# Four edits of instruction order in a two-layer decoder trunk: the sums and the rotary tables of the feed-forward, the end of the stick-breaking mixer, and 42 transposes of the identity at the start

## The chip, the cores and the metric

The kernel runs on one core of a Trainium2 chip. The metric is the device time of one execution, in microseconds (us); lower is better. A core has five instruction queues that matter here: PE (TensorE, matrix products, with its weight loads shown apart as PEld), DVE (VectorE), ACT (ScalarE), POOL (GpSimd) and SP (SyncE, which issues every DMA of this kernel). Each queue runs its instructions in the order in which they were written out when the kernel was built; an instruction waits at the head of its queue until what it reads is there and what it overwrites is free.

## The reference

Two layers over 512 tokens of width 1024, everything in float32. Layer 0 mixes tokens by retention (with rotary tables), layer 1 by stick-breaking attention. Around each mixer stand two half-step feed-forwards, and each layer ends with a gated embedding:

```python
for i in range(DEPTH):
    f = swiglu(rmsnorm(h, g[0]), w_gate[i, 0], w_up[i, 0], w_down[i, 0])
    h = h + 0.5 * rmsnorm(f, g[1])
    m = retention(...) if i % 2 == 0 else stick_breaking(...)
    h = h + rmsnorm(m, g[3])
    f = swiglu(rmsnorm(h, g[4]), w_gate[i, 1], w_up[i, 1], w_down[i, 1])
    h = h + 0.5 * rmsnorm(f, g[5])
    gate = sigmoid(rmsnorm(h, g[6]) @ ple_w_gate[i])
    h = h + rmsnorm(gate * (p[i] @ ple_w_proj[i]), g[7])
```

with `swiglu(x, ...) = (silu(x @ w_gate) * (x @ w_up)) @ w_down` and a hidden width of 2816. `rmsnorm` divides each token by the root of the mean of its squares and multiplies by a gain.

## The kernel before

**Products.** A float32 product is made of three float32r products (`mm3`, L157 to L161): each operand is split into a high part, copied by ACT (L153), and a low part, subtracted by DVE (L154). Weights come in tiles of 128x1024 (512 KB) by DMA into eight `raw` buffers, and are split into `wh` and `wl` (`piece`), of which five pairs of buffers exist (`HL_BUFS`); `_load` makes the pieces in the order of a list of items, and `_ahead` makes as many as there are free buffers. The four token tiles t = 0 to 3 hold 128 tokens each.

**Feed-forward.** `ffn` runs four times. The first hidden pair is computed plainly from four weight tiles, the other ten pairs by seven products on half-size blocks (Strassen's scheme, in Winograd's form). A pair has four raw weight tiles; products 1, 2, 3 use three of them as they are, product 4 a difference that is made late, and products 5, 6, 7 use sums of them: `t1` = raw - raw, then two more sums in place of two raw tiles. These three sums (1024 wide, on DVE, in `_load`, L247) are made just ahead of the piece of product 6, which is third in a pair's order (1, 2, 6, 5, 7, 3, 4). One product is 24 PE matmuls of 256 columns. PE adds up several products in one PSUM bank, ACT and DVE take the banks over to `y` (L687) and to the gated hidden value `u` (L748).

**Norms.** Between two parts of a layer stands a chain per token tile: DVE adds the last partial product to `part` (`close_a` for its first half, L558, and `close_b` for its second, L565), ACT squares it, POOL makes the reciprocal root (L526 to L541; it also multiplies the first half by the gain, L528), DVE multiplies the second half by the gain (L539) and adds the residual (L546), and then `pre` does the same for the next part's input norm: ACT square (L460), POOL (L451, L452), DVE `xn` (L464), PE transposes of `xn` (L470), ACT and DVE split of the transposed tile into `xs`.

**What sets the order.** A scheduler places the instructions by a model of their times; PE's order is written by hand wherever `traced()` stands. `issue_after(x)` makes what follows stand behind x on x's engine, with no wait. `chained()` gives the norm chains priority and keeps each engine's part of them in the written order. `gates` holds instructions behind which the next pieces must stand. `rope_tables` (L392 to L446) makes the sine and cosine tables with 24 DVE operations of 512 columns and three of ACT, and stores them by two DMAs that retention later reads; the scheduler puts it where it finds room. Its tiles share buffers with `xn` and `rin`.

**Start.** `run` loads the four token tiles, does `pre` for t = 0 and 1, transposes both (`flush`), sets the gates there, and then does `pre` for t = 2 and 3, whose transposes stand behind the second and the third weight tile (`_wstat_halves`).

**Stick-breaking end.** `last_products` multiplies the eight heads' outputs `oT` by the output weights. Its `product(half, t, heads)` adds some heads to the bank of one half of one token tile, one `mm3` of 512 columns for each head. In the order before, all four tiles get heads 4 to 6 of half 0, `context(7)` makes the last head, tile 0 gets heads 2 to 6 of half 1, then all four tiles get head 7 of half 0, each with its `close_a`; after that half 1 is finished tile by tile with `close_b`.

Of the kernel before, what the change touches and what calls it, by code (L numbers as in the profile page):

```python
# [18 lines left out]
P = 128  # L19
D = 1024  # L20
S = 512
NT = S // P
# [58 lines left out]
class Trunk:  # L81
# [148 lines left out]
    def piece(self, x, w, home=None):  # L230
        if home and home[0] == "blk":
            parts = [self.blk2() for _ in range(2)]
            for i, hl in enumerate(parts):
                self.split(hl, x[:, i * 512 : i * 512 + 512])
            return tuple(Parts(p) for p in zip(*parts))
        if home and home[0] in ("xe", "xs"):
            h, l = (getattr(self, home[0])[:, 2 * home[1] + i] for i in range(2))
        elif home:
            h, l = (self.work.tile([P, 1280], F32R, tag="pk", name="pk", bufs=self.npacks)[:, :w] for _ in range(2))
        else:  # L240
            h = self.hl.tile([P, 1024], F32R, tag="wh", name="wh")[:, :w]
            l = self.hl.tile([P, 1024], F32R, tag="wl", name="wl")[:, :w]
        self.split((h, l), x)
        return h, l

    def sub(self, out, a, b, op=ALU.subtract):
# [2 lines left out]
    def _load(self):  # L249
        n = self.loaded  # L250
        item = self.items[n]
        self._open(n)
        if item[0] == "w":
            x = self.packs.pop(n)
            self.queue[n] = self.piece(x, 1024, self.home.get(n))
        elif item[0] == "st":
            _, key, prod = item
            b = self.packs[key]
            if prod == 6:
                w = b[0, 0].shape[-1]  # L260
                b["t1"] = self.sums.tile([P, 1024], F32, tag="t1", name="t1")[:, :w]

                with self.tc.issue_after(self.s_sums):
                    self.sub(b["t1"], b[0, 1], b[0, 0])
                    self.sub(b[0, 0], b[1, 1], b["t1"])
                    self.sub(b[0, 1], b[1, 1], b[0, 1])
            x = {1: b[0, 0], 2: b[1, 0], 3: b[1, 1], 4: b[0, 0], 5: b.get("t1"), 6: b[0, 0], 7: b[0, 1]}[prod]
            self.queue[n] = self.piece(x, x.shape[-1])
            if prod == 6:
                self.sub(b[0, 0], b[1, 0], b[0, 0])  # L270
        self.loaded += 1
# [85 lines left out]
    def setup(self):  # L357
        nc, tc = self.nc, self.tc
        c = self.cpool


        self.part = [c.tile([P, D], F32, name=f"part{t}") for t in range(NT)]
        self.keep = [self.dram.tile([P, D], F32, name=f"keep{t}") for t in range(NT)]
        self.src = [self.ins["x"][t * P : (t + 1) * P, :] for t in range(NT)]
        self.trig = [self.dram.tile([P, 512], F32, name=f"trig{t}") for t in range(2)]
        x = self.xs.rearrange("p (t q d) (c k) -> p t q d c k", t=2, q=2, c=4)
        self.xT = [x[:, :, :, d] for d in range(2)]
        self.ident = c.tile([P, P], F32, name="ident")
        make_identity(nc, self.ident)
        self.mhalf = c.tile([P, 1], F32, name="mhalf")  # L370
        nc.gpsimd.memset(self.mhalf, -0.5)
        self.junk = c.tile([P, 512], BF16, name="junk")
        self.gng = c.tile([P, RH * RDV // P], F32, name="gng")
        self.inv = c.tile([P, 1], F32, name="inv")

    def triangle(self):
        nc = self.nc
# [307 lines left out]
    def ffn(self, layer, j, gpost, after, side=None):  # L685
# [102 lines left out]
        with self.traced():  # L788
            for n, x in enumerate(ffn_steps()):
                if n == 50 and side:  # L790
                    side()
                (gate_up if x[0] == "gu" else down)(*x[1:])
                if x[:2] == ("gu", NPAIR - 1) and x[2] in ORDER[2:]:
                    self.open_home(self.LAST[ORDER.index(x[2]) - 2])
# [191 lines left out]
    def stick(self, layer, gpost, after):  # L986
# [143 lines left out]
        h = SH - 1  # L1130

        def last_products():
# [8 lines left out]
            def product(half, t, heads):  # L1141
                for hd in heads:
                    h0 = 4 - 2 * half
                    u = (us0, us1)[half][(hd - h0) // 2]
                    self.mm3(pss[half][t], stat(hd)(0, t), [x[:, hd % 2, :] for x in u], hd == h0, hd == h)

            for t in range(NT):
                product(0, t, range(4, h))
            context(h)
            product(1, 0, range(2, h))  # L1150
            for t in range(NT):
                product(0, t, (h,))
                ssa[t] = self.close_a(t, pss[0][t], gpost, False)
            self.done_with(2)
            for t in range(NT):
                if t:
                    product(1, t, range(2, SH - 3))
                self.run_c()
# [68 lines left out]
    def run(self):  # L1227
# [10 lines left out]
        x(3)  # L1238
        nc.sync.dma_start(out=self.gng, in_=self.ins["gn"])
        nc.sync.dma_start(out=self.inv, in_=self.ins["inv"])  # L1240
        for t in range(NT):
            with self.chained():
                self.pre(t, g, True)
            self.run_d()
            if t == 1:
                self.flush()
                self.gates, self.gated = list(self.ends.values()), 3
        self.layers()
        assert self.at == len(self.items), (self.at, len(self.items))

# [99 lines left out]
```

## Time and profile before

| what | before |
|---|---|
| device time, median of 3 (range) | 2220.15 us (2218.29 to 2221.09) |
| profiled execution: its time, its span | 2220.81 us, 2218.9 us |
| mean granted PE clock in it | 0.995 |
| PE / PEld busy | 2174.7 us / 1962.7 us |
| DVE / ACT / POOL busy | 1466.0 us / 1003.4 us / 236.7 us |
| weights and activations read, written | 229.38 MB, 17.30 MB |

The profile is one execution on the chip. Rows of its timeline give the start (us from the start of the span), the duration, the engine, the line of the kernel, the operation with its output and inputs, how many equal instructions the row joins, and in square brackets how long the engine idled before and which instruction ended that. Rows of waits give the waiting engine and line, what it waited for, and the sum, the number and the longest of these waits. Rows of windows give the busy time of each engine in a stretch, the granted PE clock (PEclk, 1.00 is full speed), the share of the DMA engines and GB/s.

### The profile page before, as it was taken

How to read it: one execution, taken by the hardware profiler on the slowest of the kernel's cores; microseconds unless marked ns; L12 is line 12 of the kernel's file. 1: busy time of each engine (PE TensorE's matmuls, PEld its weight loads, DVE VectorE, ACT ScalarE, POOL GpSimd, SP SyncE). 2: the span in 40 equal slices, each digit the busy share in tenths (PEclk: the TensorE clock that was granted, in tenths of full speed). 3: DMA queues.
4: the chain of work that ended last, by engine and by line, in shares of the span. 5: the costliest groups of instructions: out<-in, count | busy, mean ns of one | idle time of the engine just before them, and what ended most of it. 6: DMA issues, size and time to landing. Idle time of an engine off the chain costs nothing.

```text
span 2218.9 us, 32989 instructions
## 1 busy us (share of the span) xinstructions
PE 2174.7 (98%) x13640; PEld 1962.7 (88%) x13640; DVE 1466.0 (66%) x1739; ACT 1003.4 (45%) x1476; POOL 236.7 (11%) x337
## 2 busy tenths in 40 slices
PE   8999999999999999999999999999999989999998
PEld 7899998888888899999988999998988889999986
DVE  7976676553535588577766976776554568767764
ACT  5543444232223355344555544444555455444443
POOL 0000003110111210000032000002131220000031
PEclk9999999999999999999999999999999999999999
DMA  5323335231322324322453233235312232333341
GB/s 214 127 102 97 106 121 181 91 106 60 110 76 81 124 96 134 114 97 94 143 201 131 87 116 112 98 103 171 115 58 77 86 115 95 105 105 105 114 162 57
DMA packets 69415, 248.83 MB, mean 112 GB/s; under 512 B 7952, under 2 KB 7952, under 8 KB 69264
## 3 DMA queue, kind: packets, MB, share of 16 engines
q1 hardware_dynamic: 69264, 246.72, 33.6%
q8 instruction: 107, 1.75, 0.3%
q14 instruction: 44, 0.36, 0.1%
HBM read 229.38 MB, written 17.30 MB: 111 GB/s over the span
## 4 chain that ended last, share of the span: by engine, by line
PE 88%; DVE 6%; ACT 2%; issue 1%; POOL 1%; DMA 1%; SPq 0%; DVEq 0%; POOLq 0%; ACTq 0%
PE ps L728 33%; PE ps L160 18%; PE ps L159 18%; PE ps L161 18%; PE ps L1042 1%; DVE wl L154 1%; DMA raw<-wts 1%; DVE raw L247 1%; DVE xs L154 1%; PE ps L470 1%; DVE part L546 0%; DVE xe L154 0%; DVE y L687 0%; ACT xn L460 0%; POOL st L541 0%
## 5 line engine op out<-in xcount | busy, mean ns | idle before, releaser
L154 DVE TENSOR_TENSOR wl<-raw,wh 128x1024 fp32r<-128x1024 f32 x427 | 526.6, 1239 | 356.2 <-ACT wh L153 353.5
L153 ACT ACTIVATE wh<-raw 128x1024 fp32r<-128x1024 f32 x427 | 449.8, 1059 | 640.5 <-PE ps L728 202.2
L728 PE MATMUL ps<-xs,wh 128*128 128x256 f32 x2560 | 464.7, 283 | 6.7 <-DVE y L687 6.6
L728 PEld LDWEIGHTS ps<-xs,wh 128*128 128x128 f32 x2560 | 399.0, 189 | 11.0 <-DVE y L687 7.9
L728 PE MATMUL ps<-xs,wl 128*128 128x256 f32 x1280 | 362.9, 284 | 0.0
L728 PE MATMUL ps<-xe,wh 128*128 128x256 f32 x1920 | 350.5, 284 | 0.0
L728 PEld LDWEIGHTS ps<-xe,wh 128*128 128x128 f32 x1920 | 302.3, 193 | 1.9
L728 PE MATMUL ps<-xe,wl 128*128 128x256 f32 x960 | 272.8, 284 | 4.3 <-DVE wl L154 4.3
L159 PE MATMUL ps<-wh,blk 128*128 128x512 f32 x680 | 266.3, 392 | 1.9 <-ACT blk L153 1.9
L161 PE MATMUL ps<-wh,blk 128*128 128x512 f32 x680 | 265.2, 391 | 1.1 <-DVE blk L154 1.1
L160 PE MATMUL ps<-wl,blk 128*128 128x512 f32 x680 | 266.0, 391 | 0.0
L728 PEld LDWEIGHTS ps<-xs,wl 128*128 128x128 f32 x1280 | 242.3, 189 | 0.0
L728 PEld LDWEIGHTS ps<-xe,wl 128*128 128x128 f32 x960 | 184.9, 193 | 4.5 <-DVE wl L154 4.5
L160 PE MATMUL ps<-xs,wh 128*128 128x256 f32 (+1 forms) x576 | 186.1, 323 | 2.2 <-DVE xs L154 2.2
L159 PE MATMUL ps<-xs,wh 128*128 128x256 f32 (+1 forms) x576 | 186.5, 324 | 0.2 <-ACT xs L153 0.2
L161 PE MATMUL ps<-xs,wl 128*128 128x256 f32 (+1 forms) x576 | 185.3, 322 | 0.0
L161 PE MATMUL ps<-wh,xs 128*128 128x512 f32 (+1 forms) x448 | 162.9, 364 | 0.0
L159 PE MATMUL ps<-wh,xs 128*128 128x512 f32 (+1 forms) x448 | 162.7, 363 | 0.0
L160 PE MATMUL ps<-wl,xs 128*128 128x512 f32 (+1 forms) x448 | 162.6, 363 | 0.0
L526 POOL TENSOR_SCALAR st<-st 128x1 f32<-128x1 f32 x32 | 8.9, 279 | 1375.0 <-ACT junk L524 1358.9
L161 PEld LDWEIGHTS ps<-wh,blk 128*128 128x128 f32 x680 | 128.0, 188 | 28.7 <-DVE blk L154 1.5
L159 PEld LDWEIGHTS ps<-wh,blk 128*128 128x128 f32 x680 | 128.2, 189 | 26.8 <-ACT blk L153 2.1
(169 smaller groups left out, 3443.8 us busy)
## 6 DMA issues: line engine op xcount, KB each, us to landing
raw<-wts SPq DMA_DIRECT2D x382, 512.0 KB, 3.5
keep<-part SPq DMA_DIRECT2D x28, 512.0 KB, 4.2
rin<-keep SPq DMA_DIRECT2D x28, 512.0 KB, 4.1
gbc<-gains SPq DMA_DIRECT2D x16, 512.0 KB, 3.8
part<-x SPq DMA_DIRECT2D x4, 512.0 KB, 7.7
rin<-x SPq DMA_DIRECT2D x4, 512.0 KB, 4.9
out<-part SPq DMA_DIRECT2D x8, 256.0 KB, 2.2
dec<-decay SPq DMA_DIRECT2D x4, 256.0 KB, 3.7
```

The source lines that it names most:

```text
L153: h = self.nc.scalar.activation(hl[0], x, AF.Copy)
L154: l = self.nc.vector.tensor_tensor(out=hl[1], in0=x, in1=hl[0], op=ALU.subtract)
L159: mm(ps, a[0], b[0], start=start, stop=False)
L160: mm(ps, a[0], b[1], start=False, stop=False)
L161: mm(ps, a[1], b[0], start=False, stop=stop)
L247: self.nc.vector.tensor_tensor(out=out, in0=a, in1=b, op=op)
L470: nc.tensor.transpose(ps[:, c * P : (c + 1) * P], xn[:, (4 * q + c) * P : (4 * q + c + 1) * P], self.ident)
L526: nc.gpsimd.tensor_scalar(out=r, in0=ss, scalar1=1.0, scalar2=(4 if half else 1) * RMS_EPS, op0=ALU.mult, op1=ALU.add)
L728: nc.tensor.matmul(o, w[a][:, g, k, :], x[b][:, k, :], start=new and g + k + n == 0, stop=k == 3 and n == 2, skip_group_check=True)
L1042: nc.tensor.matmul(ps, l, m, start=fresh and i == 0, stop=i == len(pairs) - 1, skip_group_check=True)
```

## The change

Four things are changed, and none of them changes a value that is computed. The number of instructions stays the same but for 42 transposes.

1. The three sums of a pair stand behind the low split of the piece made last before them.
2. `rope_tables` stands behind the last hidden split that was written before it.
3. `last_products` has another order, and `close_a`, `run_c`, `close_b` and `run_d` follow each other per token tile.
4. At the start PE's order is by hand: 24 transposes of the identity into a PSUM bank that nobody reads, then tile 0 is transposed, 14 more such transposes, tile 1, 4 more. `pre` of tile 1 now stands behind tile 0's transposes and their split, and the gates are taken after all four `pre`.

```diff
 def piece(self, x, w, home=None):
...
         self.split((h, l), x)
+        self.last_piece = self.split_ins[1].ins
...
 def _load(self):
...
-                with self.tc.issue_after(self.s_sums):
+                with self.tc.issue_after(self.s_sums), self.tc.issue_after(self.last_piece):
...
+    def warm(self, n):
+        ps = self.ps()
+        for i in range(n):
+            self.nc.tensor.transpose(ps[:, i % 4 * P : i % 4 * P + P], self.ident, self.ident)
...
 def ffn(self, layer, j, gpost, after, side=None):
...
                 if n == 50 and side:
-                    side()
+                    with ExitStack() as stack:
+                        for i in self.split_ins:
+                            stack.enter_context(self.tc.issue_after(i.ins))
+                        side()
...
 def last_products():
...
             for t in range(NT):
-                product(0, t, range(4, h))
+                product(0, t, (4, 5))
+            for t in range(2):
+                product(0, t, (6,))
+            product(1, 0, range(2, 6))
             context(h)
-            product(1, 0, range(2, h))
+            for t in range(2, NT):
+                product(0, t, (6,))
+            product(1, 0, (6,))
             for t in range(NT):
                 product(0, t, (h,))
+                if t == NT - 1:
+                    self.done_with(2)
                 ssa[t] = self.close_a(t, pss[0][t], gpost, False)
-            self.done_with(2)
-            for t in range(NT):
                 if t:
                     product(1, t, range(2, SH - 3))
                 self.run_c()
...
 def run(self):
...
-        for t in range(NT):
-            with self.chained():
-                self.pre(t, g, True)
-            self.run_d()
-            if t == 1:
-                self.flush()
-                self.gates, self.gated = list(self.ends.values()), 3
+        with self.traced():
+            self.warm(24)
+            for t in range(NT):
+                with self.chained():
+                    self.pre(t, g, True)
+                self.run_d()
+                if t < 2:
+                    self.flush()
+                    self.warm(14 - 10 * t)
+            self.gates, self.gated = list(self.ends.values()), 3
```

The lines of the changed kernel are numbered 1 to 15 higher; a number behind a name below tells one buffer from another.

The order of DVE at the start, before: `xn` is the normed input of a token tile (`part0` to `part3`), `wl` the low part of a weight tile.

```order
L464 SCALAR_TENSOR_TENSOR xn_127<-part0_92,st_129,gbc_113 128x1024
L464 SCALAR_TENSOR_TENSOR xn_134<-part1_93,st_136,gbc_113 128x1024
L154 TENSOR_TENSOR wl_203<-raw_116,wh_202 128x1024
L154 TENSOR_TENSOR xs_58<-ps_140,xs_58 128x4x128
L154 TENSOR_TENSOR xs_58<-ps_147,xs_58 128x4x128
L154 TENSOR_TENSOR xs_58<-ps_154,xs_58 128x4x128
L154 TENSOR_TENSOR xs_58<-ps_161,xs_58 128x4x128
L154 TENSOR_TENSOR wl_207<-raw_118,wh_206 128x1024
L154 TENSOR_TENSOR wl_211<-raw_120,wh_210 128x1024
L464 SCALAR_TENSOR_TENSOR xn_169<-part2_94,st_171,gbc_113 128x1024
L464 SCALAR_TENSOR_TENSOR xn_176<-part3_95,st_178,gbc_113 128x1024
L154 TENSOR_TENSOR wl_215<-raw_192,wh_214 128x1024
```

The same place on DVE after the change:

```order
L471 SCALAR_TENSOR_TENSOR xn_154<-part0_92,st_156,gbc_113 128x1024
L154 TENSOR_TENSOR xs_58<-ps_160,xs_58 128x4x128
L154 TENSOR_TENSOR xs_58<-ps_167,xs_58 128x4x128
L471 SCALAR_TENSOR_TENSOR xn_190<-part1_93,st_192,gbc_113 128x1024
L154 TENSOR_TENSOR wl_251<-raw_116,wh_250 128x1024
L154 TENSOR_TENSOR xs_58<-ps_196,xs_58 128x4x128
L154 TENSOR_TENSOR xs_58<-ps_203,xs_58 128x4x128
L471 SCALAR_TENSOR_TENSOR xn_216<-part2_94,st_218,gbc_113 128x1024
L471 SCALAR_TENSOR_TENSOR xn_223<-part3_95,st_225,gbc_113 128x1024
L154 TENSOR_TENSOR wl_255<-raw_118,wh_254 128x1024
L154 TENSOR_TENSOR wl_259<-raw_120,wh_258 128x1024
L154 TENSOR_TENSOR wl_263<-raw_240,wh_262 128x1024
```

The split of tile 0 now stands ahead of `xn` of tile 1, and the second, third and fourth weight tile are split behind `xn` of tile 3, where two of them stood ahead of `xn` of tile 2.

In the first feed-forward, DVE before, at the sums of pairs 1 and 2 (`t1_766` and raw 393 to 399 belong to pair 2, raw 194 to 200 and `wl_598` to pair 1; `wl_598` is the low part for product 6 of pair 1):

```order
L247 TENSOR_TENSOR t1_766<-raw_397,raw_393 128x1024
L435 TENSOR_TENSOR rope_2242<-rope_2242,rope_2244 128x512
L247 TENSOR_TENSOR blk_517<-blk_517,blk_516 128x512
L154 TENSOR_TENSOR xe_91<-blk_516,xe_91 128x4x128
L247 TENSOR_TENSOR raw_194<-raw_200,t1_593 128x1024
L247 TENSOR_TENSOR raw_198<-raw_200,raw_198 128x1024
L247 TENSOR_TENSOR raw_393<-raw_399,t1_766 128x1024
L247 TENSOR_TENSOR raw_397<-raw_399,raw_397 128x1024
L406 TENSOR_SCALAR rope_2242<-rope_2242 128x512
L154 TENSOR_TENSOR xe_91<-blk_517,xe_91 128x4x128
L687 TENSOR_TENSOR y_707<-y_707,ps_709 128x512
L154 TENSOR_TENSOR wl_598<-raw_194,wh_597 128x1024
```

The same place after the change (pair 1 has `t1_641`, raw 242 to 248 and `wl_646`; pair 2 has `t1_814` and raw 441 to 447):

```order
L248 TENSOR_TENSOR t1_641<-raw_246,raw_242 128x1024
L154 TENSOR_TENSOR xe_91<-blk_564,xe_91 128x4x128
L154 TENSOR_TENSOR xe_91<-blk_565,xe_91 128x4x128
L248 TENSOR_TENSOR raw_242<-raw_248,t1_641 128x1024
L248 TENSOR_TENSOR raw_246<-raw_248,raw_246 128x1024
L154 TENSOR_TENSOR wl_646<-raw_242,wh_645 128x1024
L154 TENSOR_TENSOR wl_683<-t1_641,wh_682 128x1024
L248 TENSOR_TENSOR raw_242<-raw_244,raw_242 128x1024
L154 TENSOR_TENSOR wl_719<-raw_246,wh_718 128x1024
L154 TENSOR_TENSOR wl_752<-raw_248,wh_751 128x1024
L694 TENSOR_TENSOR y_755<-y_755,ps_757 128x512
L154 TENSOR_TENSOR wl_783<-raw_242,wh_782 128x1024
```

Pair 2's sums and the rotary operations no longer stand between pair 1's sums and its first low part. Pair 2's `t1` is the next row after these. In the later pairs the sums stand behind the low part of the pair's own product 2 (or of a down-projection tile written just before), where some stood four to six pieces earlier. The rotary operations now stand between the pieces of a pair some 150 DVE rows further on, and the two DMAs that store the tables some 40 rows further on in SP's queue.

At the stick-breaking end, POOL before (L528 multiplies the first half of a token tile by the gain; L540 and L541 make the reciprocal root of the mixer's closing norm, L451 and L452 that of the next input norm):

```order
L526 TENSOR_SCALAR st_16719<-st_16717 128x1
L528 TENSOR_TENSOR part0_92<-part0_92,gbc_14667 128x512
L526 TENSOR_SCALAR st_16728<-st_16726 128x1
L528 TENSOR_TENSOR part1_93<-part1_93,gbc_14667 128x512
L526 TENSOR_SCALAR st_16737<-st_16735 128x1
L528 TENSOR_TENSOR part2_94<-part2_94,gbc_14667 128x512
L526 TENSOR_SCALAR st_16746<-st_16744 128x1
L528 TENSOR_TENSOR part3_95<-part3_95,gbc_14667 128x512
L540 TENSOR_TENSOR st_16758<-st_16757,st_16719 128x1
L541 TENSOR_TENSOR st_16758<-st_16758,mhalf_107 128x1
```

POOL after the change:

```order
L533 TENSOR_SCALAR st_16767<-st_16765 128x1
L535 TENSOR_TENSOR part0_92<-part0_92,gbc_14715 128x512
L547 TENSOR_TENSOR st_16775<-st_16774,st_16767 128x1
L548 TENSOR_TENSOR st_16775<-st_16775,mhalf_107 128x1
L533 TENSOR_SCALAR st_16786<-st_16784 128x1
L535 TENSOR_TENSOR part1_93<-part1_93,gbc_14715 128x512
L458 TENSOR_SCALAR st_16804<-st_16801 128x1
L459 TENSOR_TENSOR st_16804<-st_16804,mhalf_107 128x1
L547 TENSOR_TENSOR st_16819<-st_16818,st_16786 128x1
L548 TENSOR_TENSOR st_16819<-st_16819,mhalf_107 128x1
```

The reciprocal root of tile 0 stands behind one multiplication by the gain, where it stood behind four.

## The prediction

> **What bounds the kernel now.** I read the page's busy times first, then the table of waits of PE over the whole run (the sum of the waits, their number, the longest).
>
> ```profile
> span 2218.9 us, 32989 instructions
> PE 2174.7 (98%) x13640; PEld 1962.7 (88%) x13640; DVE 1466.0 (66%) x1739; ACT 1003.4 (45%) x1476; POOL 236.7 (11%) x337
> ...
> PE ps L470 <- DVE xn L464: 15.0, 4, 8.1
> PE ps L728 <- DVE y L687: 6.6, 5, 2.5
> PE ps L728 <- DVE wl L154: 4.3, 1, 4.3
> PE ps L159 <- ACT blk L153: 3.5, 5, 1.9
> PE ps L161 <- DVE blk L154: 1.1, 1, 1.1
> ```
>
> PE is busy for 98% of the span, and the change takes no product away. So an order can win only what PE idles (2218.9 - 2174.7 = 44 us, and of these 8.1 before its first work) and what it runs at a lower clock. The waits shown, 30.5 us, are nearly all of what is within reach; all four places that the change touches are among them. The clock is read from windows of 20 us:
>
> ```profile
> 60.00:80.00 20.00, 15.72 (x113) 15.51 (x112) 19.49 (x25) 10.40 (x14) 0.00 (x0) 0.83 0.32 106
> 1760.00:1780.00 20.00, 18.90 (x82) 15.70 (x82) 8.99 (x12) 6.42 (x14) 2.98 (x4) 0.91 0.31 106
> 1780.00:1800.00 20.00, 14.30 (x65) 11.45 (x64) 11.51 (x14) 6.61 (x14) 10.12 (x16) 0.91 0.45 138
> 1860.00:1880.00 20.00, 17.48 (x135) 17.28 (x134) 17.73 (x22) 8.76 (x14) 0.00 (x0) 0.92 0.34 106
> ```
>
> The eighth column is the clock. Taken as stretches at half speed these are 0.17 x 40 = 6.8 us, 3.6, 3.6 and 3.2 us; work in such a stretch loses half its length. Each stands at one of the waits below: where PE idles for some 2 us or more the clock falls, and the wait is paid a second time. I add 2.7 us for the first (1.5 of its 6.8 lie in the idle time), 1.4 and 1.6 for the two of the stick-breaking end, 1.6 for the last.
>
> **Edit 1 and 2, first feed-forward.** Around PE's longest wait in the middle of the run stand these rows of DVE and PE:
>
> ```profile
> 32.00:66.00 34.00, 6.87 (x12) 0.00 (x0) 1.00 0.10 32
> 57.65 2.37 DVE L247 TENSOR_TENSOR t<-raw 128x1024 f32<-128x1024 f32 x2
> 61.72 1.24 DVE L247 TENSOR_TENSOR raw<-raw,t 128x1024 f32<-128x1024 f32 x1
> 65.13 1.24 DVE L247 TENSOR_TENSOR raw<-raw 128x1024 f32<-128x1024 f32 x1
> 67.80 1.24 DVE L154 TENSOR_TENSOR wl<-raw,wh 128x1024 fp32r<-128x1024 f32 x1
> 69.09 0.58 PE L728 MATMUL ps<-xe,wl 128*128 128x256 f32 x1 [4.28 <-DVE wl L154]
> ```
>
> The first row is the rotary tile alone: 6.87 us of DVE in 34 us (its first number is DVE). The low part for product 6 begins at 67.80, and PE stood from 64.81 to 69.09 for it. Ahead of it stand the rotary operations and pair 2's three sums (half of the two t and of four raw rows: 3 x 1.2 = 3.6 us). Both leave this place: 6.9 + 3.6 = 10.5 us less, of which some is taken up where DVE now waits for PE's banks; even at 5 us the low part is ready before PE asks. So the wait of 4.28, a later one of 0.3 and the clock's 2.7 go: **-7.2 us**.
>
> Where the tables go, DVE has room:
>
> ```profile
> 200.00:260.00 60.00, 60.00 (x416) 56.16 (x415) 42.56 (x50) 25.50 (x34) 0.00 (x0) 1.00 0.31 98
> L410 DVE SCALAR_TENSOR_TENSOR rope<-rope x10: 686/694/706, 30.1 to 74.9; 128x512 f32<-128x512 f32 x10
> SPq L445 <- ACT rope L441: 2.6, 1, 2.6
> ```
>
> PE is busy for all 60 us there and DVE for 42.56. The tables are 10 x 0.69 and 14 shorter ones, 13 us in all, against 17.4 of slack: I cost them at nothing. If the cover fails, DVE's excess is paid at PE, 2 to 4 us; and SP's two stores wait for the last table with weight loads queued behind them (2.6 us before, the third row), which eight raw buffers cover. The bound is 0 to +4.
>
> **Edit 1, the other three feed-forwards.** Here the trace has waits of DVE for a DMA and, a few instructions later, of PE for DVE:
>
> ```profile
> 1252.26 1.23 DVE L247 TENSOR_TENSOR t<-raw 128x1024 f32<-128x1024 f32 x1 [2.55 <-DMA raw<-wts]
> 1255.27 0.51 PE L728 MATMUL ps<-xs,wh 128*128 128x256 f32 x2 [1.71 <-DVE y L687]
> 1271.31 0.50 PE L728 MATMUL ps<-xs,wh 128*128 128x256 f32 x2 [1.45 <-DVE y L687]
> ...
> DVE t L247 <- DMA raw<-wts: 2.8, 2, 2.3
> PE ps L728 <- DVE y L687: 2.5, 1, 2.5
> ```
>
> The last two rows are of 1845 to 1885. In each case a later pair's `t1` stands at the head of DVE before its weights have landed; the additions to `y` behind it come late, and PE waits for the bank that they read. Behind the change `t1` stands where its pair's product 2 is already split, so its raw tiles are due anyway. Gains: 1.71 + 1.45 = 3.2; 2.5 and the clock's 1.6; and 0.6 in the second feed-forward, what is left of the row of 6.6 (6.6 - 3.2 - 2.5 - 0.3). Sum **-7.9 us**. What is late next: the three sums and the low part follow each other just ahead of product 6, 4 x 1.22 = 4.9 us. A product is 24 matmuls at 0.12 us, 2.9 us, and five pairs of buffers let a piece be made four products ahead, 11.5 us. The chain fits with some 6 us over.
>
> **Edit 3, the stick-breaking end.** Rows of PE, DVE and POOL:
>
> ```profile
> 1759.29 0.50 PE L159 MATMUL ps<-wh,blk 128*128 128x512 f32 x1 [1.92 <-ACT blk L153]
> 1761.13 0.79 PE L161 MATMUL ps<-wh,blk 128*128 128x512 f32 x1 [1.10 <-DVE blk L154]
> 1776.97 1.30 POOL L528 TENSOR_TENSOR part<-part,gbc 128x512 f32<-128x512 f32 x1
> 1782.25 1.30 POOL L528 TENSOR_TENSOR part<-part,gbc 128x512 f32<-128x512 f32 x1
> 1777.89 0.69 DVE L565 TENSOR_TENSOR part<-part,ps 128x512 f32<-128x512 f32 x1
> 1784.36 1.28 DVE L546 SCALAR_TENSOR_TENSOR part<-part,st,rin 128x1024 f32<-128x1024 f32 x1 [3.89 <-POOL st L541]
> 1789.50 1.06 PE L470 MATMUL ps<-ident,xn 128*128 128x128 f32 x8 [3.50 <-DVE xn L464]
> 1794.86 1.97 PE L470 MATMUL ps<-ident,xn 128*128 128x128 f32 x8 [2.21 <-DVE xn L464]
> ```
>
> From tile 0's last addition (1777.89) to its transposes (1789.50) pass 11.6 us, because POOL multiplies all four tiles by the gain (1776.97 to 1783.55) ahead of the first root; DVE idles 3.89 us for that root. With one multiplication ahead of it this part shrinks by some 3.9 us to 7.7. The last addition also comes earlier: three one-head products of 0.68 us fewer ahead of it, the wait of 3.0 before head 6 cut to some 0.6 (nine more products stand before it now), and the clock's 1.4: 2.0 + 2.4 + 1.4 = 5.8, at 1772. So tile 0 is ready near 1780, where PE gets to it near 1781: no wait. Tile 1 follows 5.4 us after tile 0 before (1794.86 - 1789.50), and will be ready some 1.2 us late. Of all that PE loses here, 1.9 + 1.1 + 3.5 + 2.2 = 8.7 idle and 3.0 of clock, I leave 0.6 at head 6, 1.2 at tile 1 and 1.0 at the split behind it: **-8.9 us**. Bounds: 0 (what is late next takes it all) and -11.7 (all of it goes).
>
> **Edit 4, the start.** DVE, ACT and PE:
>
> ```profile
> 9.97 1.29 DVE L464 SCALAR_TENSOR_TENSOR xn<-part,st,gbc 128x1024 f32<-128x1024 f32 x1 [1.97 <-POOL st L452]
> 14.89 2.36 DVE L154 TENSOR_TENSOR wl<-raw,wh 128x1024 fp32r<-128x1024 f32 x2
> 15.71 1.05 ACT L460 ACTIVATE xn<-part 128x1024 f32<-128x1024 f32 x1
> 19.97 1.28 DVE L464 SCALAR_TENSOR_TENSOR xn<-part,st,gbc 128x1024 f32<-128x1024 f32 x1 [0.71 <-POOL st L452]
> 11.32 1.97 PE L470 MATMUL ps<-ident,xn 128*128 128x128 f32 x8 [1.29 <-DVE xn L464]
> 19.90 0.27 PE L159 MATMUL ps<-xs,wh 128*128 128x256 f32 x1
> 22.40 1.03 PE L470 MATMUL ps<-ident,xn 128*128 128x128 f32 x8
> ```
>
> Eight transposes take 1.97 us early and 1.03 at 22.40: PE runs at half speed until 19.9. The 42 transposes, 42 x 0.25 = 10 us at half speed, mostly fill time that PE idles (8.1 us before tile 0, and the wait for tile 1), and can bring full speed forward. But the weights are now the later ones. Tile 1's square stands behind tile 0's split: at 9.7 for 7.87, so `xn` 1 at 11.8, its transposes at 13.1 and the first product at 14.4 or so. Tiles 2 and 3 are squared one behind the other from 14.7, `xn` of tile 3 ends at 20.2, and only then comes the second `wl`: done at 21.3 where it was done at 16.1 (the row of two at 14.89). Product 1 (24 matmuls) is over by 18 at full speed and by 20 at half, so PE waits for 21.3 either way. The third weight tile then starts near 24.9 for 23.2: **+1.7 us** at full speed. As PE idles for 1 to 3 us just there, the clock is likely down after it, for up to 3.4 us more (the stretches above): another 1.7. I take **+2.5**, bounds 0 and +5.
>
> The Trainium skill, "TensorE: Matmul & The Clock Gate", part 4 (PE-mode transpose), says that transposes do not count as busy time for the clock. By that rule the 42 would change nothing but the queue, the first product would run at half speed, and the start would cost about +3.4 in place of +1.7. This trace speaks rather against it: the eight transposes from 1794.86 are 1.97 us, more than half of the 3.6 us at half speed there, and the clock was full again behind them.
>
> **Sum.** -7.2 - 7.9 - 8.9 + 2.5 = -21.5 us against the profiled execution's 2220.81, so 2199.3; the median of the three runs is 0.7 lower than that execution. Predicted: **2199 us**.
>
> **Rivals.**
> (a) *The sums just in time meet something else.* In the feed-forwards the waits for `y` move to the low part of product 6, since `t1` now also stands behind a low split that waits for a buffer. For it: DVE is busy 17.73 of 20 us at 1860 to 1880. Against it: 6 us of cover. Then edit 3 and the first feed-forward alone pay, and the tables cost 3: -8.9 - 7.2 + 2.5 + 3 = -10.6: 2210 us.
> (b) *The end's wait only moves.* Tile 1 is late by as much as tile 0 was, since DVE and ACT now interleave both halves of three tiles. The end then gives 5.8 - 2 = some 4 us: 2204 us.
> (c) *Slower.* The chain of three sums and a low part, 4.9 us, is paid in each of 40 pairs. It decides from the point where pieces are made less than two products (5.7 us) ahead; with one product ahead (2.9) it costs 2.0 a pair, 40 x 2.0 = 80 us, less the 13 that is won elsewhere: some 2286 us. At 1252 the pieces were ahead by more than that in spite of 2.55 us of waiting, so it is unlikely.
> (d) *The edits do not do what they say*: the scheduler's order keeps a wait of the same length at each of the three places, and the start costs: 2222 us.
>
> **How the numbers follow.** Forecast 0.62, (a) 0.13, (b) 0.13, (c) 0.05, (d) 0.07. The forecast's own bounds are the sum with the end at -11.7 and the start at 0 (2194) and with the start at +5 and the tables at +4 (2206). (a) and (b) reach to 2211; low 2193 and high 2212 leave out (c), (d) and little else. About 0.2%, 4.4 us, is what a measurement of this kernel can tell from no change: faster means below 2215.7. Forecast, (a) and (b) are all faster: 0.88; (d) is no change, 0.07; (c) slower, 0.05.
>
> **What would show it.** Right: no wait of PE near 65 us, none for `y` in the later feed-forwards, at the stick-breaking end tile 0's transposes near 1772 (8.5 us from the parts before, 9 here) with no wait ahead of them; POOL's first root behind one multiplication. At the start a new wait of PE for `wl` of 1 to 3 us near 18 to 21, and the third tile's transposes some 2 us later than 22.40. Wrong: a wait of PE for `wl` ahead of product 6, a wait near 200 to 260, weight loads late behind the tables' stores, or a start that is no later than before.

## The result, and the profile after

| | before | after |
|---|---|---|
| device time, median | 2219.4 us (4 runs, 2218.29 to 2221.09) | 2198.59 us (4 runs, 2197.71 to 2198.9) |
| ratio to before, 95% interval | | 0.9905 (0.9888 to 0.9922) |
| span of the profiled execution | 2218.9 us | 2196.8 us |
| PE busy; the rest of the span | 2174.7; 44.2 us | 2171.3; 25.5 us |
| DVE / ACT / POOL busy | 1466.0 / 1003.4 / 236.7 us | 1460.2 / 1002.4 / 236.7 us |

The kernel is 20.8 us faster, 0.9%. The time sits in the parts where the forecast put it. First the waits of PE over the whole run after the change (the sum, the number, the longest); L477, L735 and L572 are L470, L728 and L565 of before.

```profile
PE ps L477 <- DVE xn L471: 5.0, 3, 2.5
PE ps L161 <- DVE wl L154: 2.9, 1, 2.9
PE ps L159 <- ACT xs L153: 1.7, 2, 1.5
PE ps L159 <- ACT blk L153: 1.6, 4, 0.4
PE ps L160 <- DVE xs L154: 1.5, 6, 0.3
```

The rows of 6.6 us (for `y`) and 4.3 us (for product 6's low part) are gone, that of 15.0 us (for `xn`) is 5.0, and one is new: 2.9 us for a `wl`, at the start. To see where the 22 us of span went, I subtract the times at which the same transposes of `xn` run in the two traces; they stand at every border between parts. The row is that of tile 3, or of tile 0 where it says so; a negative number is time won:

| border | before, us | after, us | difference | made in this part | forecast |
|---|---|---|---|---|---|
| start | 27.59 | 31.38 | +3.8 | +3.8 | +2.5 |
| end of feed-forward 1 (tile 0) | 363.97 | 359.30 | -4.7 | -8.5 | -7.2 |
| end of feed-forward 2 (tile 0) | 1124.58 | 1119.09 | -5.5 | -0.9 | -0.6 |
| end of feed-forward 3 (tile 0) | 1537.38 | 1528.13 | -9.2 | -3.8 | -3.2 |
| end of stick-breaking | 1810.47 | 1792.69 | -17.8 | -8.5 | -8.9 |
| end of feed-forward 4 (tile 0) | 2143.26 | 2121.14 | -22.1 | -4.3 | -4.1 |

In the parts that the change leaves alone (retention, the two embeddings) the difference moves by less than 0.1 us; that is why a row of the fourth column can differ from the next by 0.1 more or less than the fifth says. Timeline rows of the first feed-forward after the change, and the window into which the tables moved:

```profile
59.79 1.22 DVE L248 TENSOR_TENSOR raw<-raw,t 128x1024 f32<-128x1024 f32 x1
62.86 1.23 DVE L154 TENSOR_TENSOR wl<-raw,wh 128x1024 fp32r<-128x1024 f32 x1 [0.72 <-ACT wh L153]
67.52 0.40 PE L735 MATMUL ps<-xe,wh 128*128 128x256 f32 x2
60.00:80.00 20.00, 20.00 (x162) 19.69 (x161) 18.29 (x18) 13.28 (x18) 0.00 (x0) 1.00 0.32 106
200.00:260.00 60.00, 60.00 (x424) 56.54 (x423) 51.34 (x70) 25.05 (x33) 0.00 (x0) 1.00 0.27 86
```

The low part for product 6 now begins at 62.86 (67.80 before) although the start is 3.8 us later, PE gets to that product at 67.52 and does not wait, and it is busy for all 20 us of 60 to 80 at full clock (15.72 at 0.83 before). From 200 to 260 DVE has 51.3 us of work for 42.6, and PE still idles for none of it. The stick-breaking end, on POOL, DVE and PE:

```profile
1763.38 1.29 POOL L535 TENSOR_TENSOR part<-part,gbc 128x512 f32<-128x512 f32 x1
1764.63 0.64 POOL L547 TENSOR_TENSOR st<-st 128x1 f32<-128x1 f32 x1
1762.26 0.69 DVE L572 TENSOR_TENSOR part<-part,ps 128x512 f32<-128x512 f32 x1
1763.81 1.41 DVE L546 TENSOR_TENSOR part<-part,gbc 128x512 f32<-128x512 f32 x1 [0.87 <-ACT junk L545]
1752.97 0.50 PE L161 MATMUL ps<-wh,blk 128*128 128x512 f32 x1 [0.28 <-DVE blk L154]
1771.58 1.03 PE L477 MATMUL ps<-ident,xn 128*128 128x128 f32 x8
1776.50 1.09 PE L477 MATMUL ps<-ident,xn 128*128 128x128 f32 x8 [1.15 <-DVE xn L471]
1781.15 0.38 PE L159 MATMUL ps<-xs,wh 128*128 128x256 f32 x1 [1.47 <-ACT xs L153]
1781.87 0.39 PE L160 MATMUL ps<-xs,wh 128*128 128x256 f32 x1 [0.34 <-DVE xs L154]
```

One multiplication stands ahead of the first root, tile 0's transposes have no wait, tile 1's have 1.15 us, the split behind it 1.47 and 0.34, and head 6 has 0.28 left of 3.0: 3.2 us of idle time where 8.7 stood. The start on PE:

```profile
1.41 5.05 PE L381 MATMUL ps<-ident 128*128 128x128 f32 x24 [1.41 <-POOL ident masks.py:199]
7.83 1.09 PE L477 MATMUL ps<-ident,xn 128*128 128x128 f32 x8 [1.37 <-DVE xn L471]
12.94 1.97 PE L477 MATMUL ps<-ident,xn 128*128 128x128 f32 x8 [2.48 <-DVE xn L471]
21.99 0.38 PE L161 MATMUL ps<-xs,wl 128*128 128x256 f32 x1 [2.85 <-DVE wl L154]
20.00:40.00 20.00, 18.01 (x139) 17.95 (x140) 11.65 (x14) 9.16 (x14) 0.00 (x0) 0.91 0.48 193
```

After 24 transposes of the identity tile 0's eight take 1.09 us (1.97 before), so the clock was full; tile 1's take 1.97 again, behind a wait of 2.48 us; then the second weight tile's low part holds PE for 2.85 us, and the window of 20 to 40 us has a clock of 0.91, so it fell again behind that wait.

### The profile page after: what moved, and what is told of

It is laid out like the page before. It is cut to its first block, busy times and chain, and to the rows that moved or that the text cites. A ratio compares the mean times of both kernels' runs of the same rounds, so it can differ in the third digit from the quotient of the medians.

```text
span 2196.8 us, 33031 instructions
## 1 busy us (share of the span) xinstructions
PE 2171.3 (99%) x13682; PEld 1962.0 (89%) x13682; DVE 1460.2 (66%) x1739; ACT 1002.4 (46%) x1476; POOL 236.7 (11%) x337
## 4 chain that ended last, share of the span: by engine, by line
PE 92%; DVE 3%; ACT 2%; issue 1%; POOL 1%; DMA 0%; DVEq 0%; POOLq 0%; SPq 0%; ACTq 0%
PE ps L735 36%; PE ps L159 18%; PE ps L160 18%; PE ps L161 18%; PE ps L1052 1%; PE ps L477 1%; DVE xs L154 1%; ACT xn L467 1%; DVE part L553 0%; DVE xn L471 0%; ACT xs L153 0%; PE ps L945 0%; POOL st L548 0%; POOL pk L1045 0%; ACT junk L545 0%
## 5 line engine op out<-in xcount | busy, mean ns | idle before, releaser
L735 PE MATMUL ps<-xs,wh 128*128 128x256 f32 x2560 | 462.4, 282 | 0.0
L735 PEld LDWEIGHTS ps<-xs,wh 128*128 128x128 f32 x2560 | 397.6, 189 | 3.1
L735 PE MATMUL ps<-xs,wl 128*128 128x256 f32 x1280 | 362.2, 283 | 0.0
L735 PE MATMUL ps<-xe,wh 128*128 128x256 f32 x1920 | 348.7, 283 | 0.0
L735 PEld LDWEIGHTS ps<-xe,wh 128*128 128x128 f32 x1920 | 300.7, 192 | 1.9
L735 PE MATMUL ps<-xe,wl 128*128 128x256 f32 x960 | 271.6, 283 | 0.0
L735 PEld LDWEIGHTS ps<-xs,wl 128*128 128x128 f32 x1280 | 241.3, 189 | 0.0
L735 PEld LDWEIGHTS ps<-xe,wl 128*128 128x128 f32 x960 | 183.8, 192 | 0.0
```

Of the source, the lines that this page charges most:

```text
L735: nc.tensor.matmul(o, w[a][:, g, k, :], x[b][:, k, :], start=new and g + k + n == 0, stop=k == 3 and n == 2, skip_group_check=True)
```

## The experiments

Each kernel is the changed one with the edit shown, so its time is to be held against 2198.59 us. Shifts are of the borders in the table above, against the changed kernel's trace.

**The start.** The old start:

```diff
-        with self.traced():
-            self.warm(24)
...
+            if t == 1:
+                self.flush()
+                self.gates, self.gated = list(self.ends.values()), 3
```

> The changed kernel with the start of before (no transposes of the identity, gates after tile 1). If the start is a loss because the second to fourth weight tile stand behind xn of tile 3, tile 3's transposes come at 27.6 again (31.4 with the change), everything behind is 3.8 us earlier, and the time is about 2194.8. Rival: the 42 transposes are what helps, the clock then being full sooner, and the time is 2199 or more. A third: later cover hides the start, and the shift is gone by 360 us; the time is 2198.6.

Measured: 2193.94 us (4 runs, 2193.7 to 2194.57), ratio to before 0.9886 (0.9870 to 0.9903).

```profile
26.59 1.03 PE L477 MATMUL ps<-ident,xn 128*128 128x128 f32 x8
```

Tile 3's transposes come at 26.59, 4.8 us earlier than with the change, and stay so to the end (PE's last product 4.9 us earlier). So edit 4 costs 4.7 us and nothing later hides it. The old start alone moved by 1.0 us between this trace and that of before (26.59 and 27.59): the first products reached full speed at 17.8 us in one and at 19.9 in the other, in the same order.

The new order without the transposes:

```diff
-            self.warm(24)
...
-                    self.warm(14 - 10 * t)
```

> The changed kernel without the 42 transposes of the identity, the new order of the start kept. If transposes alone raise the clock, tile 0's eight transposes take 1.97 us again (1.09 with the change), and tile 3's come some 1 to 3 us later than 31.4, since the first product runs at half speed until about 21; time 2199.5 to 2201.5. If transposes do not count for the clock, tile 0's take 1.09 us without them too, or the start is the same 31.4; time 2198.6.

Measured: 2199.56 us (one run). Rows of PE:

```profile
7.88 1.97 PE L477 MATMUL ps<-ident,xn 128*128 128x128 f32 x8 [7.88 <-DVE xn L471]
14.42 1.97 PE L477 MATMUL ps<-ident,xn 128*128 128x128 f32 x8 [4.58 <-DVE xn L471]
23.48 0.39 PE L161 MATMUL ps<-xs,wl 128*128 128x256 f32 x1 [1.67 <-DVE wl L154]
31.34 0.93 PE L477 MATMUL ps<-ident,xn 128*128 128x128 f32 x7
```

Tile 0's transposes take 1.97 us again: transposes alone do raise the clock. But tile 3's come at 31.34, the same as with all 42. The expectation of 1 to 3 us more failed for this place, though its premise held. Two things cancel in this trace. The second `wl` comes later: PE goes on at 23.48 for 21.99, mainly since ACT and DVE now split the first weight tile ahead of tile 0, an order that changed along with the edit. And behind that wait, which is shorter (1.67 for 2.85 us), PE runs on at full speed, where the changed kernel's trace has about 4 us at half speed. The total is 1.0 us higher, and that arises elsewhere: the stick-breaking end has the same waits in both traces, but here its clock falls (0.91 from 1780 to 1800, 1.00 with the change), and tile 3 is 1.5 us later behind it. So no gain of the 42 transposes shows at this start; one trace on each side can't rule out one of 1 us.

The gates one step earlier:

```diff
-            self.gates, self.gated = list(self.ends.values()), 3
+                if t == 1:
+                    self.gates, self.gated = list(self.ends.values()), 3
```

> The changed kernel with the gates taken after tile 1, so that the second and third weight tile are split between xn of tile 2 and xn of tile 3. If the order of these splits is the cost, PE's wait for the second wl shrinks from 2.85 to about 1.0 us, the clock does not fall at 23 us, and tile 3's transposes come at 28 to 29.5; time 2195 to 2196.5. If the clock or the longer chain of tile 1 is the cost, they stay at 31 and the time at 2198.6.

Measured: 2195.05 us (one run).

```profile
20.07 0.38 PE L161 MATMUL ps<-xs,wl 128*128 128x256 f32 x1 [0.81 <-DVE wl L154]
27.97 1.03 PE L477 MATMUL ps<-ident,xn 128*128 128x128 f32 x8
```

The wait for the second `wl` is 0.81 us, the clock does not fall behind it, and tile 3's transposes come at 27.97, earlier than in any of the eight traces with the changed start (29.6 to 31.5). Two low parts moved ahead of one `xn` give back 3.4 of the 3.8 us, so the order of these splits is the cost, with the fall of the clock that it brings.

The old order with 38 such transposes:

```diff
-                if t < 2:
-                    self.flush()
-                    self.warm(14 - 10 * t)
-            self.gates, self.gated = list(self.ends.values()), 3
+                if t == 1:
+                    self.flush(1)
+                    self.warm(10)
+                    self.flush()
+                    self.warm(4)
+                    self.gates, self.gated = list(self.ends.values()), 3
```

> The changed kernel with the order of before at the start (both squares first, gates after tile 1), but with 24 transposes of the identity ahead of tile 0, 10 between tiles 0 and 1 and 4 behind. If both readings hold (order is the cost, transposes raise the clock), this has the good side of both: tile 0's transposes take 1.1 us, the first two products run at full speed from about 14, tile 2's transposes come at 20.8 to 21.3 and tile 3's at 26 to 26.5 (27.6 before, 31.4 with the change); time 2193 to 2194, the fastest. If the transposes are worth nothing, it is the same as with the old start, 2194.8.

Measured: **2192.09 us** (4 runs, 2191.98 to 2193.1), ratio to before 0.9878 (0.9863 to 0.9893), the fastest of all.

```profile
7.92 1.09 PE L477 MATMUL ps<-ident,xn 128*128 128x128 f32 x8 [1.49 <-DVE xn L471]
11.20 1.09 PE L477 MATMUL ps<-ident,xn 128*128 128x128 f32 x8 [1.10 <-DVE xn L471]
19.81 1.04 PE L477 MATMUL ps<-ident,xn 128*128 128x128 f32 x8
25.00 1.03 PE L477 MATMUL ps<-ident,xn 128*128 128x128 f32 x8
```

All four tiles' transposes run at full speed, and tile 3's come 6.4 us before the changed kernel's. Against the old start without transposes (2193.94; the ranges of the two do not meet) this start is worth 1.9 us. The transposes account for it as far as the rows show: the first product no longer runs at half speed. But the two starts differ in one thing more, which no run separates: DVE splits tile 0 ahead of the first weight tile here, and behind it in the old start.

**The feed-forwards.** The sums early again, the tables late:

```diff
-                with self.tc.issue_after(self.s_sums), self.tc.issue_after(self.last_piece):
+                with self.tc.issue_after(self.s_sums):
```

> The changed kernel without edit 1: the sums of a pair are free to stand early again, the tables stay late. If the early t1 that waits for its weights is what makes PE wait for y, the three later feed-forwards lose what they won, 0.9, 3.8 and 4.3 us, and the first loses 0 to 1 us (3 x 1.14 us more ahead of the low part of product 6, which was ready 3.4 us early): time 2207 to 2209. Rival: the tables and the end shifted the weight DMAs and that alone cured the later waits; then the three lose nothing and the time stays within 1 us of 2198.6.

Measured: 2206.72 us (4 runs, 2204.87 to 2209.48), ratio to before 0.9942 (0.9925 to 0.9960). Its waits, PE from 30 us on and DVE at 1225 to 1275:

```profile
PE ps L735 <- DVE y L694: 6.3, 6, 1.7
DVE t L248 <- DMA raw<-wts: 2.8, 2, 1.5
1266.84 0.50 PE L735 MATMUL ps<-xs,wh 128*128 128x256 f32 x2 [1.75 <-DVE y L694]
```

The pair of waits is back, DVE's `t` for its weights and PE's for `y`. The four feed-forwards give back 2.0, 1.7, 2.7 and 1.5 us in this trace; the runs spread over 4.6 us where the changed kernel's spread over 1.2; that this is the DMA's doing was not tried. The median is 0.3 us below what was expected, but the shares are not as expected: the first two lost more (the first has waits for `y` of 1.4 us in sum), the last two less (the last one's wait for `y` is 1.29 us, and no clock was lost). No wait for product 6's low part is there.

The tables early again, the sums late:

```diff
                 if n == 50 and side:
-                    with ExitStack() as stack:
-                        for i in self.split_ins:
-                            stack.enter_context(self.tc.issue_after(i.ins))
-                        side()
+                    side()
```

> The changed kernel without edit 2: the tables' DVE operations stand in the first 80 us again, the sums late. Some 5 to 6 us of them stand in the busy stretch ahead of the low part of product 6, which was 3.4 us early: PE waits there 0.5 to 2.2 us, with up to 1.7 for the clock, so everything behind is 0.5 to 4 us later; time 2199 to 2202.5. If the tables alone made the wait of 4.28 us before, it is back whole with its clock, 6 to 7 us: 2205. If pair 2's sums alone made it, no wait: 2198.6.

Measured: 2201.72 us (one run); the first feed-forward is 2.8 us longer, the others unchanged.

```profile
70.58 0.39 PE L735 MATMUL ps<-xe,wl 128*128 128x256 f32 x1 [1.68 <-DVE wl L154]
PE ps L160 <- DVE xs L154: 0.5, 1, 0.5
```

The wait for product 6's low part is back with 1.68 us, and one of 0.5 for a split of `xs`. So neither the tables alone (1.68) nor pair 2's sums alone (none) make the 4.28 us of before; it took both.

**The stick-breaking end.** The new order of the heads with the two old loops:

```diff
-                if t == NT - 1:
-                    self.done_with(2)
                 ssa[t] = self.close_a(t, pss[0][t], gpost, False)
+            self.done_with(2)
+            for t in range(NT):
                 if t:
```

> The changed kernel with the new order of the products up to head 7 but the two loops of before (close_a of all four tiles, then half 1), so that POOL multiplies four tiles ahead of the first root. By the forecast's terms the end keeps the 2.4 us at head 6 and the 1.4 of the clock there, and loses the rest: tile 0's transposes at the end 4.7 us later than with the change, PE waits for them some 3.5 us again; time 2203 to 2204. If POOL's place is not what held tile 0, less than 2 us is lost.

Measured: 2202.91 us (one run), tile 0's transposes 4.4 us later than with the change.

```profile
1764.41 0.69 DVE L572 TENSOR_TENSOR part<-part,ps 128x512 f32<-128x512 f32 x1
1770.88 1.28 DVE L553 SCALAR_TENSOR_TENSOR part<-part,st,rin 128x1024 f32<-128x1024 f32 x1 [3.88 <-POOL st L548]
1776.03 1.06 PE L477 MATMUL ps<-ident,xn 128*128 128x128 f32 x8 [3.50 <-DVE xn L471]
1740.00:1800.00 60.00, 52.77 (x314) 45.79 (x313) 34.15 (x38) 26.52 (x48) 18.88 (x32) 1.00 0.42 141
```

From the last addition to the transposes pass 11.6 us again, with the same 3.88 us of DVE waiting for POOL. The clock stays at 1.00 through the end, in spite of the wait of 3.50 us.

The other half, old heads and the interleaved loop:

```diff
-                product(0, t, (4, 5))
-            for t in range(2):
-                product(0, t, (6,))
-            product(1, 0, range(2, 6))
+                product(0, t, range(4, h))
             context(h)
-            for t in range(2, NT):
-                product(0, t, (6,))
-            product(1, 0, (6,))
+            product(1, 0, range(2, h))
```

> The changed kernel with the heads in the old order (4 to 6 of all tiles, then head 7's context), but close_a and close_b of a tile following each other, the other half of edit 3. If the two halves add up, this one gives back the 2.7 us at head 6 (waits of 1.92 and 1.10 there for 0.28) and 0 to 1.7 for the clock, and keeps tile 0 without a wait: 2.5 to 4.5 us above the change, 2201 to 2203. If the interleaving does it all, it is within 1 us of 2198.6; if it needs the new order of the heads to do anything, it is near the old end, 2207.

Measured: 2202.71 us (4 runs, 2199.88 to 2204.05), ratio to before 0.9917 (0.9901 to 0.9934). The window of 1740 to 1800 and two rows of PE:

```profile
1740.00:1800.00 60.00, 53.98 (x299) 46.86 (x298) 33.91 (x38) 26.29 (x47) 18.87 (x30) 0.94 0.42 141
1749.84 0.50 PE L159 MATMUL ps<-wh,blk 128*128 128x512 f32 x1 [1.94 <-ACT blk L153]
1776.01 1.03 PE L477 MATMUL ps<-ident,xn 128*128 128x128 f32 x8
```

The wait of 1.94 us at head 6 is back, and the clock with 0.94; tile 0's transposes have no wait. The profiled execution is the slowest of the four, 2204.05; the fastest, 2199.88, has a mean clock of 0.999 for 0.996, so the clock's part of this loss varies from run to run. Its control, the whole old end:

```diff
-                product(0, t, (4, 5))
...
+                product(0, t, range(4, h))
             context(h)
...
+            product(1, 0, range(2, h))
             for t in range(NT):
                 product(0, t, (h,))
-                if t == NT - 1:
-                    self.done_with(2)
                 ssa[t] = self.close_a(t, pss[0][t], gpost, False)
+            self.done_with(2)
+            for t in range(NT):
```

> The changed kernel with the whole old end, as a control of the runs on its two halves: the end's part of the whole change (8.5 us in the two traces) comes back, 2207.1, less up to 1.7 where the clock does not fall behind the end's waits or at the start.

Measured: 2208.13 us (4 runs, 2207.63 to 2210.1), ratio to before 0.9947 (0.9933 to 0.9962): 9.5 us for the whole of edit 3. The kernels with one half each lose 4.3 us (one run) and 4.1, together 8.4: within the spread of the runs, which is 4.2 us for one of them, the two halves add up.

Last, POOL by itself: the old end, with a tile's multiplication moved to just ahead of its own root (`defer` is set for `last_products` alone).

```diff
 def post_a(self, t, g, half):
...
-        nc.gpsimd.tensor_tensor(out=a, in0=a, in1=g[:, :512], op=ALU.mult)
+        if not self.defer:
+            nc.gpsimd.tensor_tensor(out=a, in0=a, in1=g[:, :512], op=ALU.mult)
...
 def post_b(self, t, g, half, ssa, after):
...
+        if self.defer:
+            a = self.part[t][:, :512]
+            nc.gpsimd.tensor_tensor(out=a, in0=a, in1=g[:, :512], op=ALU.mult)
         nc.gpsimd.tensor_tensor(out=r, in0=ss, in1=ssa, op=ALU.add)
```

> The changed kernel with the old end whole, and only POOL's multiplication of a tile by the gain moved from close_a to just ahead of that tile's own root. If POOL's four multiplications are what held the first root, from tile 0's last addition to its transposes pass 7.7 us instead of 11.6, PE's wait of 3.5 us there is gone or under 0.3, and the end is 3.5 to 5 us shorter than before's; time 2202 to 2204. If the two loops themselves (the order of PE and ACT) set that time, it stays at 11 us or more and the time at 2207.1, the change with the old end.

> The old end with POOL's multiplication just ahead of each tile's own root, timed beside the old end itself. In one look it idled 1.85 us less than the old end of before, but the clock fell three times in the end and not twice (1.7 us). If that fall was chance, the median is 1.5 to 2 us below the old end; if the multiplications only hold up the next tile's root and DVE's xn (2.29 us for 1.28), it is within 0.7 us of it.

Measured: 2205.17 us (one run), then 2207.6 us (4 runs, 2205.91 to 2208.22), 0.5 us below the old end timed beside it. The first expectation failed, and of the second's two cases the one within 0.7 us holds. Rows of the later run, POOL, DVE and PE, and below them the row of before that the first is held against:

```profile
1773.17 0.55 POOL L552 TENSOR_TENSOR st<-st,mhalf 128x1 f32<-128x1 f32 x1
1777.11 1.59 POOL L550 TENSOR_TENSOR part<-part,gbc 128x512 f32<-128x512 f32 x1
1769.84 0.69 DVE L576 TENSOR_TENSOR part<-part,ps 128x512 f32<-128x512 f32 x1
1777.49 2.29 DVE L471 SCALAR_TENSOR_TENSOR xn<-part,st,gbc 128x1024 f32<-128x1024 f32 x1
1779.93 1.06 PE L477 MATMUL ps<-ident,xn 128*128 128x128 f32 x8 [1.96 <-DVE xn L471]
1786.56 1.09 PE L477 MATMUL ps<-ident,xn 128*128 128x128 f32 x8 [1.92 <-DVE xn L471]
```

```profile
1783.77 0.55 POOL L541 TENSOR_TENSOR st<-st,mhalf 128x1 f32<-128x1 f32 x1
```

The first root does come sooner: the power begins 3.3 us behind the last addition (1773.17 - 1769.84), where before it was 5.9 (1783.77 - 1777.89), and from that addition to tile 0's transposes pass 10.1 us for 11.6. But the next tile's multiplication now runs while DVE makes `xn`, which takes 2.29 us for 1.28, and it stands ahead of the next tile's root: tile 1 follows 6.6 us behind tile 0 (5.4 before), and the wait ahead of tile 1 is 1.92. Counted from the border ahead of this part, tile 0 comes 1.5 us earlier than in the old end's trace, and tile 3 only 0.3. So POOL's queue held the first root, as argued, but clearing it there alone is not enough. The interleaved loop, which also spreads the additions and squares of the first halves over the tiles, is enough for tile 0 (no wait in the run above); which of the things that it spreads matters was not separated.

## Why the prediction was right

**The bound.** Only PE's idle time and its clock could be won, and the gain is made of these two: the rest of the span beside PE's busy time fell from 44.2 to 25.5 us, and PE's own busy time by 3.4 us, at a mean clock of 0.998 for 0.995 and with 42 instructions more.

**First feed-forward, forecast -7.2, measured -8.5.** Right in mechanism: the long wait needed both the tables and pair 2's sums, as the two runs show. Two sizes were off. A wait of 0.54 us at 31.59, for a split that stood behind a rotary operation, was left out of the sum (the run with early tables has one of 0.5); the other 0.8 us by which the part gained more stay open. And the claim that half of the 10.5 us would do was too easy: the low part ends at 64.1 and PE asks for it near 67.5, 3.4 us in hand. That fits with the tables alone (6.9 us in before's trace) bringing a wait back, and 3.4 us of sums alone not.

**The tables at 200 to 260, forecast 0.** Right: PE idles for nothing there, with 8.7 us of DVE's slack left, and no wait of PE or DVE for a late weight stands behind the tables' stores.

**The other feed-forwards, forecast -7.9, measured -9.0.** Right: the early `t1` brings the waits back. The third won 3.8, 0.6 more than its two waits; where that 0.6 was lost before stays open. The last won 4.3, 1.8 more than its wait, where 1.6 was put down for the clock.

**The end, forecast -8.9, measured -8.5** in the two profiled executions and 9.5 by the timed control. The split was right: 0.28 us left at head 6 (0.6 forecast), 1.15 at tile 1 (1.2), 1.8 at the split behind it (1.0). The chain from last addition to transposes was mis-sized: 7.7 us forecast, 9.3 measured (1771.58 - 1762.26). It counted each step by its length alone, but DVE's multiplication beside POOL's takes 1.41 us for 0.69, and POOL's sum behind it 0.64 for 0.19, together 1.2 us. This cost nothing: tile 0's `xn` was done at 1770.93, and PE was busy with earlier work until 1771.58.

**The start, forecast +2.5, measured +3.8.** Right in sign and cause: the second to fourth `wl` behind `xn` of tile 3 (21.3 forecast for the second, 21.9 measured), a wait, and a clock that falls behind it. Most of the size is the clock's: the fall was forecast as likely and taken at half; in the changed kernel's trace it came in full. In the eight traces with this same start tile 3's transposes come at 29.6 to 31.5, by where the clock falls. Of the rule for the clock in the Trainium skill ("TensorE: Matmul & The Clock Gate", part 4, PE-mode transpose), that transposes do not count, the runs show the contrary for the float32 transposes of this kernel: tile 0's eight take 1.09 us behind 24 transposes of the identity in nine traces (1.53 in a tenth, where the clock falls during them), and 1.97 in the three traces without them.

**The rule for the clock.** The forecast priced each of before's long waits twice, since the clock fell behind every one of some 2 us or more. As a rule this did not hold. The kernel with the new heads alone waits 3.50 us and keeps 1.00, and the changed end keeps 1.00 in the changed kernel's trace and falls to 0.91 in that of the kernel without the 42 transposes, with the same waits. The terms that rested on it (2.7, 1.4, 1.6 and 1.6 us) fit before's trace; for a new order such a term is a chance and not a price.

**The total.** That it came within 0.5 us of 2199 is in part luck: the start is 1.3 us worse than forecast, the first feed-forward 1.3 and the others together 1.1 better, and the end 0.4 worse.

Of the rivals none came true. (a) fell with the low parts in time in all ten pairs of each feed-forward (no wait of PE for a `wl` or for `y` there), (b) with tile 1's 1.15 us, (c) with the feed-forwards' gains, (d) with the table above.

## What to carry to other kernels

Where one engine is busy for 98% of the span, list its gaps with their releasers, and read what stands on the releaser's queue just ahead of the late instruction: in the three places that won it was work that nobody needed yet (tables, a later pair's sums, three later tiles' gains), and the place that lost, the start, is the same thing made new: two later tiles' `xn` ahead of a weight that PE waits for. Move that work behind what is waited for, but move all of it, since clearing one queue for one tile can hand the wait to the next. What an edit that warms the clock wins depends on whether the data behind it is ready: such transposes went with 1.9 us less in one order of the splits, and with no gain that shows in another, which cost 4.7.

## What the runs showed of the hardware

- Transposes of a constant raise PE's clock: 24 of them from 1.41 to 6.46 us, and the next eight take 1.09 us for 1.97.
- A gap can cost more than its length. In before's end 5.5 us of gaps went and 8.5 us of time; the clock is 0.94 from 1740 to 1800 in the kernel with the old heads and 1.00 in that with the new heads alone, whose waits there are longer (3.5 us among them). What decides which of the two happens was not tried; traces of one and the same start differ by up to 1.9 us.
- The column of the granted clock can miss half speed at the start: it reads 1.00 for 0 to 20 us in the trace with the old start, where eight transposes take 1.97 us for 1.03 later.
- DVE's operations take longer while POOL multiplies: `xn` 2.29 us for 1.28, DVE's own multiplication by the gain 1.41 for 0.69. The Trainium skill, "SBUF — State Buffer", "Who interferes with whom", says that the two share one pair of ports, which one instruction holds at a time; these rows agree.
